# An expert stage whose matrix-engine order is written out, with whole-array work in clusters, a halved last down unit and one more raw tile

## The chip, the core and the metric

The kernel runs on one core of one Trainium2 chip. Its time is the device time of one execution in microseconds (us). The engines are TensorE (PE: matmuls; PEld: its weight loads), VectorE (DVE), ScalarE (ACT), GpSimd (POOL) and SyncE (SP), whose queue issues the loads of all weights. Lower is better; the times are medians of several runs.

## What is computed

One decoder block on 256 tokens of width 2048, with 16 meta tokens put before them: a token mixer (two attention branches, gated and merged), and after it a mixture of experts. The change touches the second part. In the reference it is

```python
g_sel = jnp.argmax(g_logits, axis=-1)                    # 1 of 4 groups for each token
top_p, top_i = lax.top_k(e_prob, TOP_K_IN_GROUP)         # 2 of the group's 4 experts
hg = jnp.einsum('td,edf->etf', t, w_gate_e)              # 16 experts, 2048 x 512 each
hu = jnp.einsum('td,edf->etf', t, w_up_e)
act = jax.nn.silu(hg) * hu * gates.T[:, :, None]
y = jnp.einsum('etf,efd->td', act, w_down_e)             # 512 x 2048 each
```

Then y is added to the residual, and a last RMS norm is taken over the rows. All is float32. The three expert matrices are 201 MB, and each is read once.

## The kernel before

**Weights.** All weights lie in DRAM as pieces of 128 x 2048 float32 (1024 KB), in the order in which they are used; 192 of them are the experts'. `Stream` (L82) hands them out. `load` (L106) issues a piece's DMA on SyncE's queue into a raw tile of the pool whose turn it is; a tile is rewritten only when what reads it is done. In the stage before the experts (L659 to L728, the output projection `wo`) the ring grows from 2 to 13 raw tiles (`MORE`, L664), and when the split pool is closed (L730) by `THIRD` = 1 more (L733): 14. In the expert stage a piece goes to PE as it is (`whole`, L125).

**Units.** The experts are taken in pairs p = 0 to 7. A pair has eight *up units* (`up_unit`, L870) and four *down units* (`down_unit`, L907), of two pieces each. Each expert holds at most 64 tokens, so its matmuls use half of the array's columns; the two of a pair of matmuls run side by side in two halves. A float32 matmul shows as two records, so that a unit has 16 records on PE. `moe_units` (L60) gives the order: the four down units of pair p - 1 stand between the up units of pair p. This order also sets that of the loads.

**Whole-array work.** Besides the units, PE has work on the full array: `gather` (L850) brings the group's tokens together, eight calls for each group of two pairs, two input chunks each, from parts that ACT and DVE make in `h_parts` (L840); `pair_map` (L821) makes the map back and the gate of each slot; `act_T` (L897) transposes the activations between the up and down units; `combine` (L920) adds a down unit's output to the residual, from a high part yh (ACT, L916) and a rest yl (DVE, L917). `combine` uses the two single PSUM tiles of `pt` and `pv`, as `pair_map` does; `act_T` uses `pt`.

**What sets the order.** The loop at L952 walks over the units. What a unit leaves to do is put off by `later` (L268) and done by `tick` (L272): `act_T` and `combine` one step after what they need. The program's order is only a priority: the framework's scheduler orders each engine's instructions by a simulation of its own, so PE's real order differs from the loop's. Each engine then works through its queue in order, as SyncE's does.

**The end.** With the last pair `combine` calls `last_sums` (L935) for each part of 512 columns: squares on ACT (L940), the product with the last gain on POOL (L941). `final_norm` (L985) takes the sums, scales the rows and stores them.

Of the kernel before, what the change touches and what calls it, by code (L numbers as in the profile page):

```python
# [8 lines left out]
F32 = mybir.dt.float32  # L9
F32R = mybir.dt.float32r  # L10
# [14 lines left out]
TAKEN = -3e38  # L25
CAP = 64
SPLITS, LOOK = 5, 3
RING, MORE, THIRD = 2, 11, 1
PIECE = 2048


# [40 lines left out]


UNITS = moe_units()
# [1 line left out]

def unit_pieces(kind, n, i):

    return (n * 12 + i, n * 12 + 4 + i) if kind == "u" else (n * 24 + 8 + i, n * 24 + 20 + i)


class Stream:  # L82
# [67 lines left out]
def hybrid_block(ctx, tc, a):  # L150
# [29 lines left out]
    def mm(out, lhsT, rhs, start, stop):  # L180
        T.matmul(out, lhsT, rhs, start=start, stop=stop, skip_group_check=True)  # L181
# [3 lines left out]
    pieces = [(W[i], PIECE) for i in range(MOE0 + 192)]  # L185
    halves = [(pieces[p], off, kp * c, False) for p, off, _, _, kp, c in HALVES]
    for u in UNITS:
        halves += [(pieces[MOE0 + i], 0, PIECE, True) for i in unit_pieces(*u)]
    st = Stream(nc, rawp, RING, splitp, halves, LOOK)


# [90 lines left out]
    def flush():  # L282
        while todo:
            tick()
# [377 lines left out]
    wr = tmp.tile([128, 16, 20], F32, name="wr")  # L662
    nc.sync.dma_start(wr, a["wr"])
    st.widen(raw2, MORE)  # L664
    hx = tmp.tile([128, 2, D], F32, name="hx")
    jq = tmp.tile([128, 128], I32, name="jq")
# [14 lines left out]
    def junk(r=128):  # L681
        return tmp.tile([128, 512], F32, name="junk", tag="junk", bufs=1)[:r]

    def y2(n):
        return tmp.tile([128, 512], F32, name="y2", tag="y2", bufs=2)

    S.activation(junk()[:, 0:1], ident[:, 0:1], AF.Sqrt)

# [178 lines left out]
    def half(e):  # L867
        return slice(64 * (e % 2), 64 * (e % 2) + 64)

    def up_unit(e, i):  # L870

        if i == 0:
            pgu[e] = psx([128, 512], "pgu")
        wg, wu = st.get()[0], st.get()[0]
        for k in range(4 * i, 4 * i + 4):
            x = XG[e // 4][k // 8][:, k % 8, (e % 4) * 64:(e % 4) * 64 + 64]
            ws = slice((k - 4 * i) * 512, (k - 4 * i) * 512 + 512)
            mm(pgu[e][half(e + 1)], x, wg[:, ws], k == 0, k == 15)
            mm(pgu[e][half(e)], x, wu[:, ws], k == 0, k == 15)
        if i == 3:  # L880
            later(0, up_out, e)

    def up_out(e):

        p = pgu.pop(e)
        if e % 2 == 0:
            act[e // 2] = moe.tile([128, 512], F32, name="act", tag="act", bufs=2)
        x = act[e // 2][half(e)]
        su = moe.tile([128, 512], F32, name="su", tag="su")[half(e)]
        S.activation(su, p[half(e + 1)], AF.Silu)  # L890
# [3 lines left out]
        if e % 2:  # L894
            later(1, act_T, e // 2)

    def act_T(p):  # L897
        q = pt([128, 4, 128], "pat")
        o = act.pop(p)
        for f in range(4):  # L900
            T.transpose(q[:, f, :], o[:, f * 128:(f + 1) * 128], ident)
        a = moe.tile([128, 4, 128], F32, name="aT", tag="aT", bufs=2)
        S.activation(a[:, 0:2, :], q[:, 0:2, :], AF.Copy)  # L903
        V.tensor_copy(a[:, 2:4, :], q[:, 2:4, :])
        aT[p] = a

    def down_unit(p, c):  # L907
# [6 lines left out]
        h = moe.tile([128, 512], F32R, name="yh", tag="yh", bufs=2)  # L914
        l = moe.tile([128, 512], F32R, name="yl", tag="yl", bufs=2)
# [4 lines left out]
    def combine(p, c, h, l):  # L920

        for t in range(2):
            q = (pv if t else pt)([128, 512], "pco")
# [3 lines left out]
            x = hh[t][:, c * 512:(c + 1) * 512]  # L927
            V.tensor_tensor(x, q, x, op=OP.add)  # L928
            if p == 7:
                last_sums(t, c)  # L930

    ssf = const.tile([128, 2, 4], F32, name="ssf")
    hgf = []

    def last_sums(t, c):  # L935

        cs = slice(c * 512, (c + 1) * 512)
        if len(hgf) <= t:
            hgf.append(unit([128, D], F32, f"hgf{t}"))
        S.activation(junk(), hh[t][:, cs], AF.Square, accum_out=ssf[:, t, c:c + 1])  # L940
        nc.gpsimd.tensor_tensor(hgf[t][:, cs], hh[t][:, cs], gfin[:, cs], op=OP.mult)  # L941

    expert_map(0)
    for k in (0, 2):
        h_parts(0, k)
    for k in range(0, 8, 2):
        gather(0, k)
        h_parts(0, k + 4)
    later(1, gate_values)
    later(2, pair_map, 0)  # L950
    nth = {}
    for kind, n, i in UNITS:  # L952
        if kind == "u":
            g, j = n // 4, n % 4 * 4 + i
            if g == 0 and j in (0, 1):
                for k in (8 + 4 * j, 10 + 4 * j):
                    gather(0, k)
                    if k < 12:
                        h_parts(0, k + 4)
            if n % 2 and i == 2 and n < 15:  # L960
                later(0, pair_map, n // 2 + 1)
            if g < 3 and j == 5:
                expert_map(g + 1)
                h_parts(g + 1, 0)
            if g < 3 and 6 <= j < 14:
                if j < 13:
                    h_parts(g + 1, 2 * (j - 5))
                gather(g + 1, 2 * (j - 6))
            if n == 13 and i == 0:
                gfin = unit([128, D], F32, "gfin")  # L970
                nc.gpsimd.dma_start(gfin, a["g_final"].to_broadcast([128, D]))
            up_unit(n, i)
        else:
            if n == 7 and i == 0:
                flush()
            down_unit(n, i)
        tick()
    flush()


    sf = const.tile([128, 2], F32, name="sf")
# [19 lines left out]
    with tc.If(more > 0):  # L1001
        with tc.tile_pool(name="fb", bufs=1) as fb:
# [16 lines left out]
            with tc.For_i(0, 16, 1) as e:  # L1019
# [22 lines left out]
                for c in range(4):  # L1042
                    y = [pj([128, 512], "pfy") for _ in range(2)]
                    nc.gpsimd.dma_start(wp, W[bass.ds(e * 12 + (MOE0 + 8 + c), 1)].rearrange("a p c -> p (a c)"))
                    for t in range(2):
                        for f in range(4):
                            mm(y[t], res[0][:, f, t * 128:(t + 1) * 128], wp[:, f * 512:(f + 1) * 512], f == 0, f == 3)
                        x = hh[t][:, c * 512:(c + 1) * 512]
                        V.tensor_tensor(x, y[t], x, op=OP.add)
            for t in range(2):  # L1050
                for c in range(4):
                    last_sums(t, c)
            final_norm()


# [5 lines left out]
def layout(i):  # L1061
# [14 lines left out]
    moe[:, 2] = f(i["w_down_e"])[0].reshape(16, 4, 128, 4, 512).transpose(0, 3, 2, 1, 4)  # L1076
    pos = np.arange(L, dtype=np.float32)[None, :]
    rope = []
    for half in (64, 32):
# [37 lines left out]
```

## Time and profile before

| | before |
|---|---|
| median of 3 runs | 1250.81 us (1250.37 to 1253.12) |
| the profiled execution | 1254.03 us |
| its span, from the first instruction to the last | 1252.4 us |
| PE busy | 1198.1 us (96%) |
| PE weight loads busy | 878.7 us (70%) |
| DVE busy | 593.5 us (47%) |
| ACT busy | 461.4 us (37%) |
| HBM read | 325.96 MB, 264 GB/s over the span |

The expert stage fills the span from about 757 us on. Matmuls overlap and their ends are modelled, so that a busy PE may still lose time at changes from one kind of work to another. The start of a matmul to the start of the next one tells more than its duration.

### The profile page before, as it was taken

The numbers are of one execution on the slowest core, as the hardware profiler recorded it, in microseconds if no ns is written. First come the engines' busy times: TensorE is split into PE (matmuls) and PEld (weight loads), VectorE is DVE, ScalarE is ACT, GpSimd is POOL, SyncE is SP. The second block draws the span as 40 slices with busy tenths as digits, with TensorE's granted clock in tenths as the row PEclk, the third lists the DMA queues.
The fourth block names the chain that finished last, engine by engine and source line by source line (L and its number), as shares of the span: only waits on it lengthen the run. The fifth ranks groups of instructions, "written<-read, shape, count | busy, mean of one in ns | idle before, by whom it ended". The sixth has DMA issues, their size and how long they took to land.

```text
span 1252.4 us, 18527 instructions
## 1 busy us (share of the span) xinstructions
PE 1198.1 (96%) x7602; PEld 878.7 (70%) x7602; DVE 593.5 (47%) x1075; ACT 461.4 (37%) x792; POOL 23.9 (2%) x31
## 2 busy tenths in 40 slices
PE   6999999999999999999999998999999999999994
PEld 6999889999999999999998875443433343333331
DVE  7768868555555655566564435232313131211212
ACT  6567644444355654444444324221211121000013
POOL 1000000000000000000000000000000000000002
PEclk9999999999999999999999998999999999999997
DMA  7554334433543444555559944999999999999992
GB/s 259 199 175 166 135 135 169 160 110 112 179 182 139 148 152 152 185 193 178 200 192 422 383 156 159 420 422 421 420 422 421 420 420 422 422 422 421 421 401 71
DMA packets 48456, 331.41 MB, mean 265 GB/s; under 512 B 5584, under 2 KB 6240, under 8 KB 9200
## 3 DMA queue, kind: packets, MB, share of 16 engines
q1 hardware_dynamic: 47088, 324.88, 66.2%
q0 software_dynamic: 1136, 5.29, 1.1%
q8 instruction: 62, 1.02, 0.3%
q14 instruction: 26, 0.21, 0.0%
q10 hardware_dynamic: 144, 0.01, 0.0%
HBM read 325.96 MB, written 4.19 MB: 264 GB/s over the span
## 4 chain that ended last, share of the span: by engine, by line
PE 92%; ACT 3%; DVE 3%; issue 1%; DMA 1%; SPq 0%; ACTq 0%
PE pj L181 50%; PE pgu L181 19%; PE py L181 10%; PE pxg L181 3%; PE pco L181 3%; PE pav L181 2%; PE pidx L181 1%; PE pqk L181 1%; ACT yh L916 1%; DVE yl L917 1%; PE prt L181 1%; DMA raw<-in_w 1%; ACT xTh L255 1%; PE psm L181 0%; DVE act L891 0%
## 5 line engine op out<-in xcount | busy, mean ns | idle before, releaser
L133 DVE TENSOR_TENSOR wlo<-raw,whi 128x1024 fp32r<-128x1024 f32 (+1 forms) x227 | 276.9, 1223 | 196.6 <-ACT whi L132 195.4
L181 PE MATMUL pj<-xTh,whi 128*128 128x256 f32 (+1 forms) x1216 | 348.0, 286 | 9.9 <-ACT xTh L255 9.9
L132 ACT ACTIVATE whi<-raw 128x1024 fp32r<-128x1024 f32 (+1 forms) x227 | 237.9, 1053 | 324.2 <-PE pj L181 297.1
L181 PE MATMUL pj<-xTl,whi 128*128 128x256 f32 (+1 forms) x1216 | 343.7, 283 | 0.0
L181 PE MATMUL pj<-xTh,wlo 128*128 128x256 f32 (+1 forms) x1216 | 342.6, 282 | 0.2 <-DVE wlo L133 0.2
L181 PE MATMUL pgu<-raw,xg 128*64 128x512 f32 x1024 | 263.2, 600 | 0.0
L181 PEld LDWEIGHTS pj<-xTh,whi 128*128 128x128 f32 x1216 | 229.5, 189 | 14.3 <-ACT xTh L255 9.9
L181 PEld LDWEIGHTS pj<-xTh,wlo 128*128 128x128 f32 x1216 | 229.1, 188 | 1.3 <-DVE wlo L133 0.5
L181 PEld LDWEIGHTS pj<-xTl,whi 128*128 128x128 f32 x1216 | 229.5, 189 | 0.7 <-issue 0.4
L181 PEld LDWEIGHTS pgu<-raw,xg 128*64 128x64 f32 x1024 | 77.8, 137 | 141.2 <-issue 137.7
L181 PE MATMUL py<-raw,aT 128*64 128x512 f32 x512 | 141.4, 603 | 0.5 <-ACT aT L903 0.5
L917 DVE TENSOR_TENSOR yl<-py,yh 128x512 fp32r<-128x512 f32 x32 | 22.1, 692 | 154.0 <-ACT yh L916 154.0
L181 PEld LDWEIGHTS py<-raw,aT 128*64 128x64 f32 x512 | 43.3, 138 | 71.1 <-issue 69.1
L916 ACT ACTIVATE yh<-py 128x512 fp32r<-128x512 f32 x32 | 19.1, 598 | 158.8 <-PE py L181 101.7
L891 DVE SCALAR_TENSOR_TENSOR act<-pgu,gsl,su 64x512 f32<-64x512 f32 x16 | 12.0, 750 | 98.7 <-ACT su L890 98.7
L890 ACT ACTIVATE su<-pgu 64x512 f32<-64x512 f32 x16 | 9.5, 592 | 131.5 <-PE pgu L181 131.5
L846 ACT ACTIVATE hsh<-hx,rh 128x256 fp32r<-128x256 f32 x64 | 30.4, 500 | 71.1 <-PE pxg L181 65.6
L847 DVE SCALAR_TENSOR_TENSOR hsl<-hx,rh,hsh 128x256 fp32r<-128x256 f32 x64 | 29.3, 479 | 49.0 <-ACT hsh L846 49.0
L181 PE MATMUL pj<-whi,mTh 128*128 128x512 f32 x128 | 51.0, 398 | 0.0
L181 PE MATMUL pj<-whi,mTl 128*128 128x512 f32 x128 | 50.5, 395 | 0.0
L181 PE MATMUL pj<-wlo,mTh 128*128 128x512 f32 x128 | 50.5, 394 | 0.0
L928 DVE TENSOR_TENSOR hx<-pco,hx 128x512 f32<-128x512 f32 x64 | 41.2, 686 | 18.5 <-PE pco L181 18.2
(293 smaller groups left out, 1389.4 us busy)
## 6 DMA issues: line engine op xcount, KB each, us to landing
raw<-in_w SPq DMA_DIRECT2D x303, 1024.0 KB, 15.7
hx<-in_x POOLq DMA_DIRECT2D x2, 1024.0 KB, 13.3
hTd<-y POOLq DMA_DIRECT2D x8, 256.0 KB, 5.5
out_dram<-hgf SPq DMA_DIRECT2D x8, 256.0 KB, 4.2
xr<-in_xT SPq DMA_DIRECT2D x3, 544.0 KB, 8.5
raw<-in_w SPq DMA_DIRECT2D x4, 256.0 KB, 7.0
raw<-in_w SPq DMA_DIRECT2D x2, 512.0 KB, 8.6
gfin<-in_g_final POOLq DMA_DIRECT2D x1, 1024.0 KB, 10.0
```

Source lines behind the costliest of these rows:

```text
L132: self.nc.scalar.activation(hi[:, c], src[:, c], AF.Copy)
L133: self.nc.vector.tensor_tensor(lo[:, c], src[:, c], hi[:, c].bitcast(F32), op=OP.subtract)
L181: T.matmul(out, lhsT, rhs, start=start, stop=stop, skip_group_check=True)
L255: S.activation(h, x, AF.Copy, scale=g)
L846: S.activation(h[:, t, :], x, AF.Copy, scale=rh[:, t:t + 1])
L847: V.scalar_tensor_tensor(l[:, t, :], x, rh[:, t:t + 1], h[:, t, :].bitcast(F32), op0=OP.mult, op1=OP.subtract)
L890: S.activation(su, p[half(e + 1)], AF.Silu)
L891: V.scalar_tensor_tensor(x, p[half(e)], gsl[e // 2][half(e)], su, op0=OP.mult, op1=OP.mult)
L916: S.activation(h, y, AF.Copy)
L917: V.tensor_tensor(l, y, h.bitcast(F32), op=OP.subtract)
L928: V.tensor_tensor(x, q, x, op=OP.add)
```

## The change

1. A context fixes PE's order in the expert stage to the order in which the program writes its instructions. The other engines are ordered by the scheduler as before. `later` and `tick` are not used in this stage any more.
2. The loop is rewritten by pairs. `beside(p)` lists the whole-array work of a pair in six clusters; `whole(k)` runs cluster k between two units, and makes the parts for the gathers of the next cluster. The order of the units is that of `moe_units` as before.
3. For pair 0 two gathers stand before each of the four up units of its first expert; before, four gathers were asked for ahead of the loop, and two more before each of the first two units.
4. The last down unit (pair 7, columns 1536 to 2047) is done in two halves of 256 columns, each with its own two loads of 512 KB, its own combine and its own last sums. For this the down weights lie in DRAM as (half, f, column) instead of (f, column), and the matmul of any down unit of 512 columns reads two runs of 256.
5. `THIRD` is 2: 15 raw tiles. The room comes from `act` and `aT`, with one buffer each instead of two, and from `wr`, `jq` and `y2`, which move to a pool that is closed before the expert stage.

```diff
-RING, MORE, THIRD = 2, 11, 1
+RING, MORE, THIRD = 2, 11, 2
...
-    return r
+    return r[:-1] + [("h", 7, 6), ("h", 7, 7)]
...
+    ph3 = ExitStack()
+    wot = ph3.enter_context(tc.tile_pool(name="wot", bufs=1, side="right"))
+    wr = wot.tile([128, 16, 20], F32, name="wr")
...
+    ph3.close()
     ph0.close()
...
 def up_unit(e, i):
...
-        if i == 3:
-            later(0, up_out, e)
...
-            act[e // 2] = moe.tile([128, 512], F32, name="act", tag="act", bufs=2)
+            act[e // 2] = moe.tile([128, 512], F32, name="act", tag="act", bufs=1)
...
-        a = moe.tile([128, 4, 128], F32, name="aT", tag="aT", bufs=2)
+        a = moe.tile([128, 4, 128], F32, name="aT", tag="aT", bufs=1)
...
-    def down_unit(p, c):
+    def down_unit(p, c, n=512):
-        w = st.get()[0], st.get()[0]
-        y = pj([128, 512], "py")
+        w = [st.get()[0].rearrange("p (h f c) -> p f h c", f=4, c=256) for _ in range(2)]
+        y = pj([128, n // 256, 256], "py")
...
-                mm(y[half(e)], aT[p][:, f, half(e)], w[e][:, f * 512:(f + 1) * 512], f == 0, f == 3)
+                mm(y[half(e)], aT[p][:, f, half(e)], w[e][:, f], f == 0, f == 3)
...
-        later(1, combine, p, c, h, l)
+        yhl[p, c] = h, l
...
+    def beside(p):
+        r = [[] for _ in range(7)]
+        if p:
+            r[0].append((act_T, p - 1))
+            for c in range(4):
+                r[2 + c].append((combine, p - 1, c, 512 * c))
+        r[2 if p == 0 else 5] += [(pair_map, 0)] if p == 0 else []
+        if p < 7:
+            r[5].append((pair_map, p + 1))
+        if p % 2 and p < 7:
+            r[0].append((expert_map, p // 2 + 1))
+            for i, k in enumerate((1, 1, 2, 2, 3, 4, 5, 5)):
+                r[k].append((gather, p // 2 + 1, 2 * i))
+        return r
+    written = tc.manual_schedule(engines={mybir.EngineType.PE})
+    written.__enter__()
     expert_map(0)
...
+    h_parts(0, 0)
+    h_parts(0, 2)
+    for p in range(8):
+        work = beside(p)
+        def whole(k):
+            for f, *x in work[k]:
+                f(*x)
+            for f, *x in work[k + 1]:
+                if f is gather:
+                    h_parts(*x)
+        def up(e, i):
+            if e == 0:
+                for k in (4 * i, 4 * i + 2):
                     gather(0, k)
                     if k < 12:
                         h_parts(0, k + 4)
+                if i == 1:
+                    gate_values()
+            up_unit(e, i)
+            if i == 3:
+                up_out(e)
...
+        up(2 * p, 0)
+        whole(0)
+        for i in range(3):
+            up(2 * p, i + 1)
+            down(i)
+            whole(i + 1)
+        up(2 * p + 1, 0)
+        down(3)
+        whole(4)
+        up(2 * p + 1, 1)
+        up(2 * p + 1, 2)
+        whole(5)
+        up(2 * p + 1, 3)
+    act_T(7)
+    down_unit(7, 0)
+    down_unit(7, 1)
+    combine(7, 0, 0, 0)
+    down_unit(7, 2)
+    combine(7, 1, 512, 1)
+    down_unit(7, 6, 256)
+    combine(7, 2, 1024, 2)
+    down_unit(7, 7, 256)
+    combine(7, 6, 1536, 3)
+    combine(7, 7, 1792, 4)
+    written.__exit__(None, None, None)
```

## Rows read from the trace of the kernel before

**Rows 1.** Waits of PE, 784 to 1240: who waited for whom, us, times, longest.

```profile
PE pco L181 <- ACT yh L916: 11.6, 17, 0.7
PE pat L901 <- DVE act L891: 5.2, 7, 1.5
PE pco L181 <- DVE yl L917: 2.6, 12, 0.2
...
PEld pgu L181 <- DMA raw<-in_w: 0.9, 3, 0.4
```

**Rows 2.** Windows: length, busy PE, PEld, DVE, ACT, POOL (count), clock, DMA share, GB/s.

```profile
768.00:772.00 4.00, 4.00 (x27) 2.48 (x26) 2.49 (x7) 2.46 (x7) 0.00 (x0) 1.00 0.17 33
772.00:776.00 4.00, 4.00 (x21) 1.34 (x20) 2.33 (x6) 3.04 (x6) 0.00 (x0) 1.00 0.95 375
776.00:780.00 4.00, 4.00 (x22) 1.79 (x24) 0.66 (x3) 0.00 (x0) 0.00 (x0) 1.00 0.91 340
780.00:784.00 4.00, 4.00 (x22) 1.36 (x20) 0.00 (x0) 0.24 (x1) 0.00 (x0) 1.00 0.99 371
...
784.00:1209.00 425.00, 408.15 (x1782) 155.95 (x1778) 104.64 (x197) 57.25 (x118) 0.54 (x1) 1.00 1.01 421
...
1208.50:1212.10 3.60, 1.65 (x10) 0.54 (x7) 0.81 (x2) 2.46 (x4) 0.00 (x0) 1.00 1.02 423
1212.10:1215.50 3.40, 3.40 (x8) 1.00 (x10) 0.38 (x1) 0.00 (x0) 0.00 (x0) 0.50 1.02 424
```

**Rows 3.** Waits of SyncE's queue, 784 to 1206.

```profile
SPq L113 <- DMA raw<-in_w: 135.5, 89, 2.1
```

**Rows 4.** SyncE's issues in the timeline; time to landing, 1196 to 1206 and whole stage.

```profile
748.31 0.33 SPq L113 DMA_DIRECT2D raw<-in_w  x1
...
770.30 1.66 SPq L113 DMA_DIRECT2D raw<-in_w  x2
...
1203.97 0.33 SPq L113 DMA_DIRECT2D raw<-in_w  x1
...
raw<-in_w SPq DMA_DIRECT2D x4, 1024.0 KB, 19.8
...
DMA to landing us min/median/max: 4.8/18.0/21.4
```

**Rows 5.** Timeline of PE, 925 to 937: start, us, what, count.

```profile
925.53 1.02 PE L181 MATMUL py<-raw,aT 128*64 128x512 f32 x2
926.48 0.39 PE L181 MATMUL pxg<-St,hsh 128*128 128x256 f32 x1
...
927.63 3.65 PE L181 MATMUL py<-raw,aT 128*64 128x512 f32 x14
...
932.06 0.73 PE L181 MATMUL pco<-yh,SgT 128*128 128x512 f32 x2
...
933.35 3.65 PE L181 MATMUL pgu<-raw,xg 128*64 128x512 f32 x14
```

**Rows 6.** Pieces of the chain that ended last, and PE's timeline at 762.

```profile
758.49 3.74 PE pxg L181 x18
...
762.16 1.08 PE L181 MATMUL pgu<-raw,xg 128*64 128x512 f32 x4
...
1102.97 0.66 PE pat L901 x4
...
1157.72 0.66 PE pat L901 x4
```

**Rows 7.** Timeline of the tail, 1195 to 1240.

```profile
1198.96 10.51 PE L181 MATMUL pgu<-raw,xg 128*64 128x512 f32 x46
...
1212.07 6.20 PE L181 MATMUL py<-raw,aT 128*64 128x512 f32 x18 [0.47 <-ACT aT L903]
...
1237.02 1.29 DVE L928 TENSOR_TENSOR hx<-pco,hx 128x512 f32<-128x512 f32 x2 [0.60 <-PE pco L181]
...
1239.32 0.16 DVE L986 TENSOR_REDUCE sf<-ssf 128x2 f32<-128x8 f32 x1 [1.01 <-ACT junk L940]
```

More of the change, by code (lines that the diff above doesn't have):

```diff
@@ L70, in moe_units @@
         r += up[6:]
-    return r
+    return r[:-1] + [("h", 7, 6), ("h", 7, 7)]
 UNITS = moe_units()
 def unit_pieces(kind, n, i):
-    return (n * 12 + i, n * 12 + 4 + i) if kind == "u" else (n * 24 + 8 + i, n * 24 + 20 + i)
+    if kind == "u":
+        return [(n * 12 + i, 0, PIECE), (n * 12 + 4 + i, 0, PIECE)]
+    if kind == "d":
+        return [(n * 24 + 8 + i, 0, PIECE), (n * 24 + 20 + i, 0, PIECE)]
+    return [(n * 24 + 12 * e + 8 + i // 2, i % 2 * PIECE // 2, PIECE // 2) for e in range(2)]
 class Stream:
@@ L187, in hybrid_block @@
     for u in UNITS:
-        halves += [(pieces[MOE0 + i], 0, PIECE, True) for i in unit_pieces(*u)]
+        halves += [((W[MOE0 + i][:, o:o + n], n), 0, n, True) for i, o, n in unit_pieces(*u)]
     st = Stream(nc, rawp, RING, splitp, halves, LOOK)
@@ L665, in hybrid_block @@
     hx = tmp.tile([128, 2, D], F32, name="hx")
-    jq = tmp.tile([128, 128], I32, name="jq")
+    jq = wot.tile([128, 128], I32, name="jq")
     nc.gpsimd.iota(jq, pattern=[[1, 128]], base=0, channel_multiplier=-1)
@@ L684, in y2 @@
     def y2(n):
-        return tmp.tile([128, 512], F32, name="y2", tag="y2", bufs=2)
+        return wot.tile([128, 512], F32, name="y2", tag="y2", bufs=2)
     S.activation(junk()[:, 0:1], ident[:, 0:1], AF.Sqrt)
@@ L893, in up_out @@
             S.activation(su[0:64, 0:1], ident[0:64, 0:1], AF.Sqrt)
-        if e % 2:
-            later(1, act_T, e // 2)
     def act_T(p):
@@ L905, in act_T, with combine @@
         aT[p] = a
-    def down_unit(p, c):
-        w = st.get()[0], st.get()[0]
-        y = pj([128, 512], "py")
+    def down_unit(p, c, n=512):
+        w = [st.get()[0].rearrange("p (h f c) -> p f h c", f=4, c=256) for _ in range(2)]
+        y = pj([128, n // 256, 256], "py")
         for f in range(4):
             for e in range(2):
-                mm(y[half(e)], aT[p][:, f, half(e)], w[e][:, f * 512:(f + 1) * 512], f == 0, f == 3)
-        h = moe.tile([128, 512], F32R, name="yh", tag="yh", bufs=2)
-        l = moe.tile([128, 512], F32R, name="yl", tag="yl", bufs=2)
+                mm(y[half(e)], aT[p][:, f, half(e)], w[e][:, f], f == 0, f == 3)
+        h = moe.tile([128, 512], F32R, name="yh", tag="yh", bufs=2)[:, :n]
+        l = moe.tile([128, 512], F32R, name="yl", tag="yl", bufs=2)[:, :n]
+        y = y.rearrange("p h c -> p (h c)")
         S.activation(h, y, AF.Copy)
         V.tensor_tensor(l, y, h.bitcast(F32), op=OP.subtract)
-        later(1, combine, p, c, h, l)
-    def combine(p, c, h, l):
+        yhl[p, c] = h, l
+    yhl = {}
+    def combine(p, c, at, last=None):
+        h, l = yhl.pop((p, c))
+        n = h.shape[-1]
         for t in range(2):
-            q = (pv if t else pt)([128, 512], "pco")
+            q = (pv if t else pt)([128, n], "pco")
             ts = slice(t * 128, t * 128 + 128)
@@ L926, in combine, with last_sums @@
             mm(q, SgT[p][:, ts], l, False, True)
-            x = hh[t][:, c * 512:(c + 1) * 512]
+            x = hh[t][:, at:at + n]
             V.tensor_tensor(x, q, x, op=OP.add)
-            if p == 7:
-                last_sums(t, c)
-    ssf = const.tile([128, 2, 4], F32, name="ssf")
+            if last is not None:
+                last_sums(t, last, at, n)
+    ssf = const.tile([128, 2, 5], F32, name="ssf")
     hgf = []
-    def last_sums(t, c):
-        cs = slice(c * 512, (c + 1) * 512)
+    def last_sums(t, i, at, n):
+        cs = slice(at, at + n)
         if len(hgf) <= t:
             hgf.append(unit([128, D], F32, f"hgf{t}"))
-        S.activation(junk(), hh[t][:, cs], AF.Square, accum_out=ssf[:, t, c:c + 1])
+        S.activation(junk()[:, :n], hh[t][:, cs], AF.Square, accum_out=ssf[:, t, i:i + 1])
         nc.gpsimd.tensor_tensor(hgf[t][:, cs], hh[t][:, cs], gfin[:, cs], op=OP.mult)
-    expert_map(0)
[L944 to L956, printed above, removed]
+    def beside(p):
[14 more added lines that the diff above has]
+    written.__enter__()
+    expert_map(0)
+    h_parts(0, 0)
[11 more added lines that the diff above has]
+                for k in (4 * i, 4 * i + 2):
                     gather(0, k)
@@ L959, in hybrid_block, with down @@
                         h_parts(0, k + 4)
[L960 to L978, printed above, removed]
+                if i == 1:
[3 more added lines that the diff above has]
+                up_out(e)
+        def down(c):
+            if p:
+                down_unit(p - 1, c)
+        if p == 6:
+            gfin = unit([128, D], F32, "gfin")
+            nc.gpsimd.dma_start(gfin, a["g_final"].to_broadcast([128, D]))
+        up(2 * p, 0)
[23 more added lines that the diff above has]
+    written.__exit__(None, None, None)
     sf = const.tile([128, 2], F32, name="sf")
@@ L1046, in hybrid_block @@
                         for f in range(4):
-                            mm(y[t], res[0][:, f, t * 128:(t + 1) * 128], wp[:, f * 512:(f + 1) * 512], f == 0, f == 3)
+                            mm(y[t], res[0][:, f, t * 128:(t + 1) * 128], wp.rearrange("p (h f c) -> p f h c", h=2, f=4)[:, f],
+                               f == 0, f == 3)
                         x = hh[t][:, c * 512:(c + 1) * 512]
                         V.tensor_tensor(x, y[t], x, op=OP.add)
+            V.memset(ssf, 0.0)
             for t in range(2):
                 for c in range(4):
-                    last_sums(t, c)
+                    last_sums(t, c, c * 512, 512)
             final_norm()
```

3 lines of the change are left out of this document (1 added, 2 removed).

## The prediction

> **What bounds the kernel now.** I read three views in this order: the waits of the matrix engine (PE), the windows with their DMA rates, and the issue times of the weight pieces. The waits say that in the expert stage PE hardly ever waits for weights: 0.9 us in all; it waits for yh and yl (11.6 and 2.6) and for act (5.2) [rows 1]. So the chain that ends last is PE's own, in an order that makes it wait for the pieces that it has just produced. The windows say that the DMA engines are as full: from 784 to 1209 they move 421 GB/s at a share of 1.01 [rows 2], and SyncE's queue issues a piece when an earlier one has landed (135.5 us in 89 waits) [rows 3]. A piece is 1.049 MB, so one lands every 1.049/0.421 = 2.49 us, and 19.8 us from issue to landing [rows 4] is eight pieces in flight. The last piece is issued at 1203.97 [rows 4], and lands at about 1223.8. Of the span of 1252.4 us, 28.6 follow that landing, because PE still has some units to do.
>
> So two limits lie close together. PE's order can be bettered by as much as it lags; after that the weights set the end, at their last landing plus a tail.
>
> **PE inside the stage.** A unit is 16 matmuls on half arrays, 14 of them in 3.0 us of starts (3.65 less the drain), so 3.43 us [rows 5]. A change to whole-array work costs: two py matmuls from 925.53 to 926.48 are 0.95 where 0.43 is the work, so 0.52 lost going in; the eight gather matmuls then take 1.15 until the next unit starts, of which I count 0.2 as lost going out (0.12 a matmul are left) [rows 5]. There are 64 such changes, counted along PE's timeline from the first units [rows 6] to the last combine (its add at 1237.02 [rows 7]); the written order has 47 by the loops of the diff: 4 in the first pass, 6 in passes 1, 3 and 5, 5 in passes 2, 4, 6 and 7, 5 at the end. That is 17 x 0.72 = 12 us. The waits for yh, yl and most of those for act go too, since a whole unit or more stands between a down unit and its combine, and between up_out and act_T: another 17 of 19.4 [rows 1]. New is a stall where pair_map takes the two PSUM tiles that the last combine has just filled: two adds of DVE, 1.29 together [rows 7], partly under the last matmuls: some 1.0 us in each of 7 passes, 7 us. PE alone would save 12 + 17 - 7 = 22 us.
>
> Check by a pass without gathers: 12 x 3.43 = 41.2, five clusters at 0.72 = 3.6, four combines of 1.29 - 0.2 = 1.1 [rows 5], 4.4, the transposes 0.66 [rows 6] and the maps about as much, stall 1.0: 51.5 us. Between two act_T now there are 1157.72 - 1102.97 = 54.8 [rows 6]. The weights of a pass need 24 x 2.49 = 59.8. So PE gets ahead of the weights, before the last pass, and then waits for them. The last up unit ends at 1209.5 now [rows 7]; PE alone would end it near 1188, the weights (below) allow 1203.9. Only 5.6 of the 22 us are needed to make the weights the bound.
>
> **The weights.** One more raw tile: one piece more is loaded before the first unit frees anything. Now the last such piece is issued at 748.31, and the next one at 770.30 [rows 4], so the tile costs nothing there and the stream after it is shorter by one piece: 2.5 us. Its lower end is 0, if the tile comes free late (it lies partly where y2 and wr were, which the router reads to the end); the pause of 22 us speaks for the full value. The tiles given up for it (a second act and aT) are rewritten a pass later, after their readers; they cost nothing, or, were that cover gone, a copy's wait of about a us a pass, inside PE's spare.
>
> The start: now 18 gather matmuls run from 758.49, the first unit begins at 762.16 [rows 6], is broken by more gathers, and ends at 770.3, when its tiles are filled anew [rows 4]. With two gathers before each of the first four units, the first ends at 762.2 + 3.6 = 765.8, the next ones each 3.43 + two gathers at 0.93 + a cluster 0.72 later, with some wait for copies: 772.2, 778.4, and 785.6 with pair_map. Data flow 1.4 us after an issue (a rate of 33 GB/s up to 772 for an issue at 770.30 [rows 2, 4]). Two pieces take 4.98, so the queue runs dry three times, and is continuous from 787.0 with 14.9 us of data moved: as if from 772.1. Now the four windows to 784 hold 4.48 MB, 10.6 us of data: as if from 773.4 [rows 2]. Gain 1.3 us, between -2 (late copies) and +3 (no gaps).
>
> So the last landing, T, is 1223.8 - 2.5 - 1.3 = 1220.0.
>
> Halving the last piece adds two transfers of the same total. With eight in flight a fixed cost of a transfer is hidden; I take nothing. Alone, a piece needs 4.8 us to land [rows 4], so 2.3 beside its data: 4.6 us for two is the upper end. The Trainium skill, DMA: Bandwidth & Descriptors, section Bandwidth, asks for at least 1 MiB in a DMA and puts lone 1 MB transfers at 341 GB/s. The trace differs for a full queue, with 421 GB/s. The reordered down weights make PE read two runs of 256 columns; no row shows that read. Between nothing and an entry of a cluster (0.52) for each of 32 units I take nothing; it lies in PE's spare, except 2 us in the last four units.
>
> **The tail.** With the weights as the bound, the last up unit's pieces land at T - 8 x 2.49 = T - 19.9; it ends at T - 16.2. From there to the first down unit is 1212.07 - 1209.47 = 2.6 [rows 7], as now, since act_T has nothing to hide behind: T - 13.6. That unit now takes some 5.4 us because the granted clock is 0.50 (1.2 GHz) from 1212.1 to 1215.5, after a gap in which PE was busy for 1.65 of 3.6 us [rows 2]; I keep this: T - 8.2. Then down 1 (3.6), combine 0 (0.52 + 1.29 [rows 5] = 1.8), down 2, combine 1, a half unit (1.8), combine 2, the last half (1.8): T + 8.0, the pieces being there each time. Combine of the first half 1.3; the last half's yh, yl and combine hide partly behind it, and its two adds of half size end at T + 11; squares, T + 11.7. From sf at 1239.32 [rows 7] to the end of the span are 13.1 us that stay. End: T + 24.8, against 28.6: 3.8 us, of which the order gives most (no yh and yl wait between down units) and the halves about 1. Its bounds: 5.7 with the clock at full, 1.5 with the two-run reads and later squares.
>
> **Sum.** 2.5 + 1.3 + 3.8 = 7.6 us. The profiled execution took 1254.03 (span 1252.4 and 1.6 around it), so 1246.4 on its scale. It stands 3.2 above the median of 1250.81; off the median the sum gives 1243.2.
>
> **Rivals.**
> PE stays the bound: if it gains under 5.6 us, the tail alone helps. From the end of the last up unit the new tail is 16.2 + 24.8 = 41.0 against 42.9 now, so 1.9, and the gain of PE on top: 1243.3 to 1248.9, say 1247. For it: PE never waits for weights now; against: 22 us worked out for 5.6 needed.
>
> Slower: written order makes each late operand stop everything behind it. Its place is each cluster, 42 of them before the last up unit. To end 2.5 us later than now, that unit must end at 1213.9, 26 us over my 1188: 0.62 us of stall in each cluster more than assumed, that is, an add of DVE waited for in full. At 0.8 us in each, 34 us, it ends at 1222, 12.5 later than now; less 1.9 of the tail that is 10.6, or 1261.4. Against: operands are a unit old (3.4 us and more), and PE's waits for them are 0.7 us at the longest even now [rows 1].
>
> The clock falls: a PE that waits for weights is granted 1.2 GHz more often. A unit of 3.43 then takes up to 6.9 (twice); but a unit's slot is 4.98, so it lags, has no more gaps, and is at full clock again, as at 1215.5. One more such spell at the end costs 1.9: 1245.1. The Trainium skill, TensorE: Matmul & The Clock Gate, section Why this matters for your kernels, warns of idle gaps between bursts of matmuls; the trace agrees, with the 0.50 after a gap.
>
> Halves land late, by 4.6 us: 1247.8. The extra tile is not there early, so that this part doesn't do what it says: 1245.7.
>
> **Chances.** What a measurement can tell from no change is about 0.2%, 2.5 us: faster is below 1248.3. Weights the bound, as summed: 0.58. PE the bound: 0.15, a third of it within 0.2%. Stalls: 0.10, slower. The clock: 0.06. The tile late: 0.05. Halves late: 0.06, half of it within 0.2%. So faster 0.58 + 0.10 + 0.06 + 0.05 + 0.03 = 0.82, same 0.08, slower 0.10. The range: the upper ends give 2.5 + 3 + 5.7 = 11.2 us, 1239.6, and 1238.0 with room for the spread of runs; at the other end it takes in PE as the bound for all but its worst case, the late tile and the late halves, to 1248.5. It leaves out the stalls.
>
> **What the profile would show.** PE waiting for raw in the last passes, tens of us instead of 0.9; about 47 changes of array use; waits of pco for yh and yl near nothing; first issue after the pause near 766; last landing near 1220, and 25 us from it to the end. Wrong if PE still shows no wait for raw (PE is the bound), if pgs, psgt or pco show long waits for DVE (stalls), or if DMA's share drops below 1 between 800 and 1200 (the first passes starve the queue).

## The result, and the profile after

The changed kernel takes 1243.17 us (median of 4 runs, 1242.56 to 1243.49); the kernel before 1251.96 (4 runs, 1250.37 to 1254.11). The ratio given with the result is 0.9925 with an interval of 0.991 to 0.9939: 8.8 us faster, on the predicted 1243.2. The profiled executions are 1254.03 and 1243.3 (spans 1252.4 and 1241.6), 10.7 apart where the sum of the prediction said 7.6. The runs of the kernel before fall into two groups by their mean granted clock, 1250.4 to 1251.7 us at 0.991 (17 of the 48 timed beside the experiments) and 1253.1 to 1255.3 at 0.988 to 0.990 (31), and its profiled execution, at 0.988, is of the second, so that part of the 10.7 is clock. So the forecast holds, but its terms need a second look.

First the pages: of the changed kernel the span and the chain that ended last by engine, then that chain of the kernel before.

```profile
span 1241.6 us, 18595 instructions
...
PE 69%; DMA 26%; DVE 2%; ACT 1%; issue 1%; SPq 0%; ACTq 0%
...
PE 92%; ACT 3%; DVE 3%; issue 1%; DMA 1%; SPq 0%; ACTq 0%
```

DMA's share goes from 1% to 26%: now a quarter of the span, some 320 us of the expert stage, runs over the arrival of weights. PE's waits in the stage, from 784 to 1242 (who waited for whom, us, times, longest), answer to [rows 1]:

```profile
PE py L185 <- DMA raw<-in_w: 6.9, 12, 1.3
PE pgu L185 <- DMA raw<-in_w: 4.2, 7, 0.7
PE psgt L835 <- DVE hx L936: 1.9, 6, 0.3
PE pat L904 <- DVE act L896: 1.5, 1, 1.5
PE pgs L185 <- DVE hx L936: 1.0, 6, 0.2
...
PEld py L185 <- DMA raw<-in_w: 20.2, 17, 2.2
PEld pgu L185 <- DMA raw<-in_w: 14.2, 14, 1.6
```

The waits of pco for yh and yl are gone, and act_T waits for act once, at the end. In their place the matmuls wait for raw for 11.1 us and their weight loads for 34.4, where it was 0.9 in all. psgt and pgs, which is pair_map behind the last combine, wait 1.9 + 1.0 us over six passes, 0.5 in each; in the kernel before the same two waits were 1.0 + 0.5.

The windows (length, busy PE, PEld, DVE, ACT, POOL, clock, DMA share, GB/s) answer to [rows 2]: the start of the stage, its whole, and the last landing.

```profile
768.00:772.00 4.00, 4.00 (x26) 2.59 (x26) 2.15 (x6) 2.43 (x6) 0.00 (x0) 1.00 0.59 227
772.00:776.00 4.00, 4.00 (x28) 2.45 (x24) 0.77 (x3) 1.01 (x3) 0.00 (x0) 1.00 0.94 344
776.00:780.00 4.00, 4.00 (x22) 1.47 (x21) 1.99 (x6) 1.42 (x4) 0.00 (x0) 1.00 0.99 416
780.00:784.00 4.00, 4.00 (x27) 2.76 (x29) 2.78 (x9) 2.69 (x7) 0.00 (x0) 1.00 0.93 352
784.00:788.00 4.00, 4.00 (x22) 1.40 (x20) 1.16 (x3) 1.61 (x2) 0.00 (x0) 1.00 0.80 291
784.00:1209.00 425.00, 409.09 (x1808) 170.30 (x1806) 103.37 (x201) 60.42 (x123) 0.54 (x1) 1.00 1.01 419
...
1220.00:1224.00 4.00, 4.00 (x31) 2.42 (x32) 2.87 (x6) 2.31 (x7) 3.14 (x3) 1.00 0.00 0
```

The stream of weights is as full as before over the stage (419 GB/s, 421 before), but it starts and ends earlier: 227 GB/s where it was 33, and nothing after 1220. The last landing, T, is at 1220.20 (1223.74 before). The 10.7 us between the two profiles are therefore 3.5 before the last landing and 7.2 behind it: 21.4 from T to the end of the span, 28.6 before.

### The profile page after: what moved, and what is told of

The parts are those of the page before. It is cut to its first block, busy times and chain, and to the rows that moved or that the text cites. A ratio compares the mean times of both kernels' runs of the same rounds, so it can differ in the third digit from the quotient of the medians.

```text
span 1241.6 us, 18595 instructions
## 1 busy us (share of the span) xinstructions
PE 1193.2 (96%) x7622; PEld 895.5 (72%) x7622; DVE 588.6 (47%) x1078; ACT 461.5 (37%) x797; POOL 24.4 (2%) x33
## 4 chain that ended last, share of the span: by engine, by line
PE 69%; DMA 26%; DVE 2%; ACT 1%; issue 1%; SPq 0%; ACTq 0%
PE pj L185 50%; DMA raw<-in_w 26%; PE pgu L185 6%; PE py L185 3%; PE pav L185 2%; PE pxg L185 2%; PE pqk L185 1%; PE pidx L185 1%; PE pco L185 1%; PE prt L185 1%; PE psm L185 0%; PE ppt L573 0%; DVE wlo L137 0%; PE ppt L571 0%; PE pvt L494 0%
## 5 line engine op out<-in xcount | busy, mean ns | idle before, releaser
L185 PE MATMUL pgu<-raw,xg 128*64 128x512 f32 x1024 | 245.3, 599 | 4.2 <-DMA raw<-in_w 4.2
L185 PEld LDWEIGHTS pgu<-raw,xg 128*64 128x64 f32 x1024 | 84.2, 137 | 135.1 <-issue 104.3
L185 PE MATMUL py<-raw,aT 128*64 128x512 f32 (+1 forms) x528 | 132.5, 583 | 7.4 <-DMA raw<-in_w 6.9
L936 DVE TENSOR_TENSOR hx<-pco,hx 128x512 f32<-128x512 f32 (+1 forms) x66 | 43.6, 670 | 186.2 <-PE pco L185 186.0
L920 ACT ACTIVATE yh<-py 128x512 fp32r<-128x512 f32 (+1 forms) x33 | 19.3, 584 | 196.1 <-PE py L185 196.1
L921 DVE TENSOR_TENSOR yl<-py,yh 128x512 fp32r<-128x512 f32 (+1 forms) x33 | 22.0, 667 | 59.4 <-ACT yh L920 59.4
L853 ACT ACTIVATE hsh<-hx,rh 128x256 fp32r<-128x256 f32 x64 | 30.4, 501 | 30.5 <-PE pxg L185 15.2
L185 PE MATMUL pj<-yah,whi 128*128 128x256 f32 x128 | 36.4, 284 | 0.0
L185 PE MATMUL pj<-yal,whi 128*128 128x256 f32 x128 | 35.9, 280 | 0.0
## 6 DMA issues: line engine op xcount, KB each, us to landing
raw<-in_w SPq DMA_DIRECT2D x6, 512.0 KB, 15.5
```

Of the source, the lines that this page charges most:

```text
L853: S.activation(h[:, t, :], x, AF.Copy, scale=rh[:, t:t + 1])
```

## The experiments

My theory after the result: from about 860 to 920 us on (the chain that ended last runs over landings from 857, PE's first waits for raw come after 900) the weights set the pace and the end, the written order gave PE some tens of us that it doesn't need, and the end is T plus a tail. The rival: PE is still the bound in most of the stage, and its waits for raw are small change. A second question is which part earned what. "Before" was timed again beside each group of runs: 1253.57 beside e1 to e4, 1253.49 beside e5 to e7, 1253.26 beside e8 to e11. The ratios of e1 to e11 are against it, that of the change against the 1251.96 of its own runs.

| run | median us | ratio (interval) | first gather | T | T to the end |
|---|---|---|---|---|---|
| before | 1253.3 to 1253.6 | | 758.49 | 1223.74 | 28.6 |
| the change | 1243.17 | 0.9925 (0.9910 to 0.9939) | 759.88 | 1220.20 | 21.4 |
| e1, one tile less | 1245.03 | 0.9937 (0.9924 to 0.9950) | 759.61 | 1222.27 | 21.5 |
| e2, last unit whole | 1241.15 | 0.9900 (0.9887 to 0.9914) | 758.17 | 1217.85 | 22.0 |
| e3, scheduler's order | 1251.52 | 0.9988 (0.9976 to 1.0000) | 759.67 | 1218.77 | 30.4 |
| e4, two experts abreast | 1241.74 | 0.9911 (0.9897 to 0.9924) | 759.93 | 1218.55 | 21.5 |
| e5, gathers twice | 1243.74 | 0.9930 (0.9913 to 0.9948) | 759.81 | 1220.76 | 21.4 |
| e6, gathers four times | 1272.22 | 1.0154 (1.0138 to 1.0171) | 760.16 | 1247.68 | 22.7 |
| e7, old loop, order fixed | 1249.91 | 0.9975 (0.9967 to 0.9984) | 758.10 | 1222.90 | 25.3 |
| e8, constants as before | 1240.37 | 0.9903 (0.9888 to 0.9918) | 757.22 | 1216.59 | 21.9 |
| e9, before, constants 32 bytes more | 1255.82 | 1.0023 (1.0011 to 1.0034) | 760.13 | 1224.14 | 28.3 |
| e10, e4 and e8 together | 1240.37 | 0.9900 (0.9885 to 0.9915) | 758.43 | 1216.11 | 23.0 |
| e11, the change again | 1243.21 | 0.9925 (0.9912 to 0.9939) | 759.29 | 1220.26 | 21.2 |

The last three columns are from each run's one profile, so a difference of a few tenths in them is not to be leaned on.

### Is a raw tile worth a piece?

```diff
-RING, MORE, THIRD = 2, 11, 2
+RING, MORE, THIRD = 2, 11, 1
```

> The changed kernel with 14 raw tiles instead of 15, the rest as it is. Theory (the weights set the end from the middle of the stage on): one piece more has to come after the pause, so the last landing and the end move by 2.49 us, from 1243.2 to 1245.7; PE waits for raw as long as before, some 30 to 45 us. Rival (PE's order sets the end, the tile is beside the point): 1243.2, the last landing unchanged against the end.

T is 2.1 us later and the time 1.9 longer, with the tail unchanged; counted from the first gather, which was 0.3 earlier, T is 2.3 later. So the extra tile is worth nearly the 2.5 us of a piece, although it is not free early: its first piece is issued only at 756.3, but the stream stands still until 768.3 anyway. It also says that T, and not PE, sets the end.

### How much can PE lose?

The loop in gather runs its matmuls again for all groups but the first (the products are written over with the same values).

```diff
-        for i in range(2):
+        for i in [0, 1] * (2 if g else 1):
```

> The changed kernel with each gather of groups 1 to 3 computed twice over on PE (the second time into the same PSUM tile, with the same result): 24 gathers, 8 matmuls of 0.12 us more in each, 22 us more of PE work in passes 1, 3 and 5. Theory (PE has more to spare than that, since it waits for raw for 30 us and more): 1243.2 to 1244.5, and the waits for raw fall by about 22 us. Rival (PE sets the end): 1265.

With e6 the same line has 4 in place of 2.

> The same, computed four times over: 67 us more of PE work. Theory: the spare is used up, waits for raw near nothing, and the end moves by what is over: 67 less 35 to 45, so 1265 to 1275. Rival (PE sets the end): 1310. A second rival (what PE waits for is not the weights but something else that grows with its work): no such knee between this run and the last.

e5 adds 192 matmuls at some 0.117 us, 22 us of PE, and the time stays: 1243.74 against 1243.17. PE's and its weight loads' waits for raw halve. The waits of e5 in the stage:

```profile
PE py L185 <- DMA raw<-in_w: 3.5, 7, 0.7
PE pgu L185 <- DMA raw<-in_w: 1.9, 3, 0.7
...
PEld py L185 <- DMA raw<-in_w: 10.3, 9, 1.6
PEld pgu L185 <- DMA raw<-in_w: 5.7, 6, 1.6
```

e6 adds 67 us, and the time grows by 29.1; of the waits for raw 1.8 us are left (a row of PEld), and the DMA share in the stage falls to 0.95, because now PE frees tiles too late. So PE has 67 - 29 = 38 us to spare in the changed kernel, and the rival is out: 22 us more work on PE cost 0.6 us on the median, and two of e5's four runs lie at 1243.6 and 1243.7.

### Is it the order or the fixing of it?

e3 takes away the three lines of the manual schedule, so that the same program is put in order by the framework's scheduler.

```diff
-    written = tc.manual_schedule(engines={mybir.EngineType.PE})
-    written.__enter__()
...
-    written.__exit__(None, None, None)
```

> The changed program, clusters, 15 tiles and halves, but PE's order left to the scheduler as in the kernel before. Theory (PE has some 15 us to spare before the weights cease to be the bound): it loses PE time, shows fewer waits for raw, but still some; the end moves by what the tail loses, 1 to 4 us: 1244 to 1247. Rival (fixing the order is all of the gain in the stage): PE is the bound again, no waits for raw, 1248 to 1250.

e7 is the kernel before, with its own loop and its planner, and only the order fixed as it issues.

```diff
+    written = tc.manual_schedule(engines={mybir.EngineType.PE})
+    written.__enter__()
     expert_map(0)
...
     flush()
+    written.__exit__(None, None, None)
```

> The kernel before, with its own loop, its 14 tiles and its whole last unit, but PE's order fixed to the order in which that program is written. Theory (weights bound once PE gains over 5 us): PE waits for raw appear, the end gains what the weights allow without the tile (no 2.5) and without the halves (no 2.3) : 1246 to 1249 against 1252. Rival (the clusters are what counts; without them the old order fixed makes PE stall as much as it gains): 1251 to 1255.

e3 loses nearly everything: 1251.52, more than theory and rival allowed, no wait of PE for raw (its weight loads 1.4 us), 30.4 us behind T, though T itself is 1.4 us earlier than in the change. e7 gains 3.6 us of the 8 to 10, between the two ranges. So the written order gains nothing to speak of unless it is fixed, and fixing the old one isn't enough. What the scheduler does to the order, a timeline of PE shows, first of e3 (start, us, what, count):

```profile
923.54 1.02 PE L185 MATMUL pgu<-raw,xg 128*64 128x512 f32 x2
924.50 0.73 PE L185 MATMUL pco<-yh,SgT 128*128 128x512 f32 x2
...
925.78 3.65 PE L185 MATMUL pgu<-raw,xg 128*64 128x512 f32 x14
929.27 1.02 PE L185 MATMUL py<-raw,aT 128*64 128x512 f32 x2
```

and then of e7 at the same place of the program, and in its last up unit:

```profile
922.11 3.65 PE L181 MATMUL pgu<-raw,xg 128*64 128x512 f32 x16
925.59 3.60 PE L181 MATMUL py<-raw,aT 128*64 128x512 f32 x16
929.93 0.50 PE L181 MATMUL pco<-yh,SgT 128*128 128x512 f32 x1 [0.73 <-ACT yh L916]
930.65 0.50 PE L181 MATMUL pco<-yl,SgT 128*128 128x512 f32 x1 [0.22 <-DVE yl L917]
...
1203.09 3.65 PE L181 MATMUL pgu<-raw,xg 128*64 128x512 f32 x14 [1.00 <-DMA raw<-in_w]
```

A down unit is eight matmuls and 16 records, so a matmul has two; two matmuls of a pair run beside each other on the array's halves. The scheduler lets one matmul of a pair, the lone x2, go ahead of the whole-array work and leaves its partner behind it. The lone one takes 923.54 to 924.50, 0.96 us, and the 14 others still take 3.5, what a whole unit of 16 takes in e7: 922.11 to 925.59. So each cut costs about 0.9 us. Ahead of whole-array work a lone x2 stands 18 times in the timeline of before, 18 times in e3, and never in e7 or in the change.

A second cost of the scheduler's order is the clock. In the kernel before a combine right behind its unit waits for yh and yl, and pair_map behind it for DVE's adds; after such a run of waits the granted clock fell in the middle of the stage:

```profile
1088.00:1092.00 4.00, 3.63 (x13) 1.53 (x15) 1.42 (x5) 0.00 (x0) 0.00 (x0) 0.65 1.01 422
1092.00:1096.00 4.00, 4.00 (x20) 1.36 (x18) 0.00 (x0) 0.00 (x0) 0.54 (x1) 0.92 1.01 420
```

That is 0.35 and 0.08 of 4 us, 1.7 us of PE. The profile of e3 has it at 1016 to 1024 (0.82 and 0.76) and 1140 to 1148 (0.68 and 0.90); those of e7 and of the change have no window of 4 us below 0.95 between 768 and their last matmul. Where PE is the bound, this counts in full: e3's times follow the mean granted clock of the run, from 1253.88 at 0.985 over 1250.7 to 1251.9 at 0.988 to 1246.57 at 0.991. So about 5 of the 8.3 us that its median loses go with the clock; that one causes the other is read from these numbers and not tried.

Why e7 doesn't gain more: the weights already bound it. Its last up unit waits 1.00 us for raw in the last row above, its matmuls wait for raw for 2.4 us and their weight loads for 10.4 in the stage, and T counted from the first gather is 464.8, as good as before's 465.3, because it has neither the extra tile nor the change's start. It gains behind T, 25.3 us for 28.6; and beside the executions of before at the clock of 0.991 (1250.4 to 1251.0) its 1249.91 gains under 1 us, so that most of the 3.6 is clock. PE isn't far ahead there: the planner puts a combine right behind its unit, the other two rows, and with the order fixed pco waits for yh and yl 30.3 us in the stage (14.2 in [rows 1]), which eats most of the 18 x 0.9 = 16 us that the whole pairs give. The old loop, fixed, with the tile and the new start was not run; so how much of the change's gain needs the clusters, and not only whole pairs, isn't shown.

### The last unit in halves

```diff
-    return r[:-1] + [("h", 7, 6), ("h", 7, 7)]
+    return r
...
-    ssf = const.tile([128, 2, 5], F32, name="ssf")
+    ssf = const.tile([128, 2, 4], F32, name="ssf")
...
-    down_unit(7, 6, 256)
-    combine(7, 2, 1024, 2)
-    down_unit(7, 7, 256)
-    combine(7, 6, 1536, 3)
-    combine(7, 7, 1792, 4)
+    down_unit(7, 3)
+    combine(7, 2, 1024, 2)
+    combine(7, 3, 1536, 3)
```

> The changed kernel with the last down unit whole again (one unit of 512 columns, two pieces, one combine). Theory (the halves shorten what follows the last landing): the last landing stays within 0.5 us of 1220.2; after it a unit of 3.5 instead of 1.9, then yh, yl, combine and adds of full size: sf some 2.3 us later, 1245.5. Rival (two more transfers and one more cluster eat it up): 1243.2 or less.

Against my expectation the kernel with the last unit whole is faster, 1241.15. The tail behaves: 22.0 against 21.4, so the halves do bring 0.6 us there. The loss is at the other end: the first gather of e2 starts at 758.17, 1.7 us before that of the change, in code that neither edit touches. From the first gather to T it takes 459.7 us, and the change 460.3. Two things were undone at once, the halves and the size of ssf, which is one of the constants at the bottom of the memory. The next pair takes them apart.

### Thirty-two bytes of constants

e8 is the change, with ssf (five columns) in a part of another constant tile that is long read by then, and a dummy of the old size in its place; e9 is the kernel before, with the larger tile and four columns of it used; e11 is the change, run once more beside them.

```diff
-    ssf = const.tile([128, 2, 5], F32, name="ssf")
+    V.memset(const.tile([128, 2, 4], F32, name="ssf"), 0.0)
+    ssf = cols[:, 40:50].rearrange("p (t c) -> p t c", t=2)
```

> The changed kernel whole, but with the ten sums of squares in unused columns of the tile cols, and the tile ssf kept at the size it had before (4 columns a half instead of 5), so that no tile on the left side of SBUF is shifted. Theory (the fifth column of ssf moved every tile after it, and PE's stream in the stages before the experts runs some 1.6 us slower for it): the first gather starts near 758.2 instead of 759.9, the end moves by as much: 1241.4. Rival (it is the 20 more PE instructions or the two more loads of the halves that delay the earlier stages): first gather at 759.9 and 1243.2.

```diff
-    ssf = const.tile([128, 2, 4], F32, name="ssf")
+    ssf = const.tile([128, 2, 5], F32, name="ssf")[:, :, 0:4]
```

> The kernel before with one edit: ssf has 5 columns a half, of which 4 are used as before. Theory (the shift of the tiles after it costs 1.6 us in the earlier stages): the first gather starts near 760.0 instead of 758.5, the wlo matmuls of the projections take some 2.5 us more in all, the time is 1.5 to 2 us over that of the kernel before. Rival (the instructions of the halves cost it): no change.

> The changed kernel once more, on the chip of these runs, to compare with: 1243.2, first gather at 759.9, last landing at 1220.2 and 21.4 from there to the end, no spell of half clock in the tail.

Eight bytes a partition more in ssf (32 as the framework pads its tiles, which no run shows by itself) cost the kernel before 0.23% (2.6 us on its median), and taking them out of the change gives 2.8: 1240.37 against 1243.21. The 2.8 may hold more than the constants: in e8's profile T also comes 0.9 us sooner behind the first gather, as the clock is back earlier there, which the part on the prediction takes up. The cost can be seen in one row of the page, matmuls of the stages before the experts (busy us and mean ns behind the bar). Of e8, with the constants as before, and of e9, with 32 bytes more:

```profile
L185 PE MATMUL pj<-xTh,wlo 128*128 128x256 f32 (+1 forms) x1216 | 342.5, 282 | 0.5 <-DVE wlo L137 0.5
```

```profile
L181 PE MATMUL pj<-xTh,wlo 128*128 128x256 f32 (+1 forms) x1216 | 345.0, 284 | 0.0
```

The same row is between 342.5 and 342.9 in the five kernels with the smaller tile (before, e2, e7, e8, e10), and between 344.9 and 345.6 in the eight with the larger. PE's order isn't the reason: up to the first gather the 5602 records of matmuls stand in the same order in before and e9, and in the change and e8. No row says which tile's new address does it.

### Filling the gaps at the start

The first pass takes its units two experts abreast, so that the gathers of an input block serve two units and frees come more evenly.

```diff
+        if p == 0:
+            r += [("u", e, i) for i in range(4) for e in range(2)]
+            continue
...
+        if p == 0:
+            for i in range(4):
+                if i == 3:
+                    pair_map(0)
+                up(0, i)
+                if i == 3:
+                    pair_map(1)
+                up(1, i)
```

> The changed kernel with the first pair's two experts taken abreast: up units (0,0), (1,0), (0,1), (1,1) and so on, the loads in the same order, so that two units and not one stand after each two gathers. Theory (the weights set the end, and the queue ran dry three times between 768 and 788): the DMA windows from 772 on are full, the last landing comes 2.5 to 4.5 us earlier, 1238.7 to 1240.7. Rival (PE sets the end): the work of PE is the same, 1243.

> Both edits that helped: the first pair's experts abreast and the sums in cols. Theory: the two gains (1.5 and 1.7) add up against the changed kernel: 1240.0, the last landing near 1217, 21.5 from there to the end. Rival (they overlap, as both let the weights start earlier): 1241.5.

In e4 the windows that ran at 344, 416, 352 and 291 GB/s in the change are full (columns as above):

```profile
772.00:776.00 4.00, 4.00 (x26) 2.47 (x27) 2.46 (x6) 2.42 (x6) 0.00 (x0) 1.00 1.01 424
776.00:780.00 4.00, 4.00 (x22) 1.40 (x20) 0.00 (x0) 0.00 (x0) 0.00 (x0) 1.00 1.02 426
780.00:784.00 4.00, 4.00 (x28) 2.48 (x26) 1.46 (x4) 2.01 (x6) 0.00 (x0) 1.00 1.01 422
784.00:788.00 4.00, 4.00 (x22) 1.31 (x20) 0.99 (x3) 0.42 (x2) 0.00 (x0) 1.00 1.01 422
```

T comes 1.65 us earlier, where I had expected 2.5 to 4.5, and the time is 1.4 us shorter, which is once more the weights as the bound. With e8 on top (e10) T counted from the first gather is again 1.7 earlier than in e8 (457.7 against 459.4), but the median is e8's, 1240.37, and the profile has a longer tail, 23.0. Its windows:

```profile
1198.00:1202.60 4.60, 2.66 (x15) 1.22 (x13) 0.90 (x2) 2.46 (x4) 0.00 (x0) 1.00 1.02 424
1202.60:1206.10 3.50, 3.50 (x10) 1.05 (x12) 0.28 (x1) 0.00 (x0) 0.00 (x0) 0.51 1.00 417
```

In this execution the first down unit met a granted clock of 0.51, 1.2 GHz, as in [rows 2]; that it is why e10 gains nothing over e8 isn't shown, and stays open: its two runs at a mean clock of 0.991 took 1239.66 and 1239.99, the two below 1240.75 and 1240.82, and e8's four, none below 0.991, lie between 1239.61 and 1241.31. Its first gather was also 1.2 us later than e8's. The best versions are e8 and e10, 1% under the kernel before and 2.8 us under the change.

## Why the prediction was right, step by step

**The weights become the bound.** Right, and with more room than I gave it. I put PE's saving at 22 us for 5.6 needed; the end of the last up unit came forward by 5.5 (1209.5 to 1203.95), and e6 shows 38 more in hand, so it is some 43. I counted the changes of array use rightly (47 for 64, by PE's timeline), and a light pass takes 48.6 us between two act_T (860.53 to 909.14) where I had 51.5 (54.8 before).

My reading of SyncE's queue was half of it. [rows 3] shows only its waits for landings; in the same stretch, 784 to 1206, it waited longer for PE to free a tile. The change turns that over. First before, then the change:

```profile
SPq L113 <- PE pgu L181: 166.2, 90, 7.9
SPq L113 <- PE py L181: 48.4, 23, 4.2
...
SPq L117 <- DMA raw<-in_w: 293.6, 142, 3.5
SPq L117 <- PE pgu L185: 49.5, 23, 5.5
SPq L117 <- PE py L185: 15.9, 18, 2.6
```

The DMA share was 1.01 either way, so the sum didn't suffer from it.

**The step that was mis-sized: "so 0.52 lost going in".** I took the two py records at 925.53 [rows 5] for one pair's work of 0.43 and a drain of 0.52. They are two records of one matmul whose partner was left for later, 2 x 0.43 and 0.1 beside it; the 14 others take 3.48, as a full unit does. The price of a real change stands in the timeline of the change, behind a unit of 16:

```profile
871.47 3.60 PE L185 MATMUL py<-raw,aT 128*64 128x512 f32 x16
875.00 0.51 PE L185 MATMUL pco<-yh,SgT 128*128 128x512 f32 x1
```

From 871.47 to 875.00 are 3.53 us for 3.43 of starts: 0.1 for going in. So 17 changes fewer are worth little (17 x 0.3 with the 0.2 going out, 5 us, not 12), and 18 cut pairs mended are worth 16. The waits for yh, yl and act that went are 15.5 up to the last up unit (the 17 that I counted take in the tail's), and pair_map's stall grew by 1.4 us, from 1.5 to 2.9 in all, and not by 1.0 in each pass. With the 1.7 of half clock at 1088 to 1096 that makes some 37 of the 43; the other 6 I have not itemised. The same error made the tail too long, below. The order of size was right for the wrong reason; the 3.43 of a unit stands, though it was read from such a run of 14. The two prices are read from timelines; no run changes the number of switches alone.

**The weights' term.** T was to be 1220.0 and is 1220.20, but by two errors that cancel. The stage begins 1.4 us later than before (first gather 759.88, not 758.49), which I had not foreseen: it is the constants, as e9 shows with 1.6. From the first gather T comes 4.9 us earlier, not 3.8. The tile gave 2.3 (e1; 2.5 predicted). The rest is the start: the five windows from 768 to 788 hold 6.52 MB, 15.5 us at 421 GB/s, so the stream is as if from 772.5, 12.6 us behind the first gather, where it was 773.4 and 14.9: 2.3 us, not 1.3. The first issue after the pause is at 768.26, 8.4 behind the first gather, where I had 7.3 (765.8). The 1.0 is the clock: the gathers and the first 2.1 us of the first unit ran at a granted clock of 0.50, 1.2 GHz (0.79 is the mean of 764 to 768, so it rose at about 765.7). I hadn't carried that beyond the gathers; the unit took 4.60 us (763.57 to 768.17) and not 3.6. In e8 the clock was back as the unit began, and it took 3.58. The change, its window, and e8:

```profile
763.57 4.67 PE L185 MATMUL pgu<-raw,xg 128*64 128x512 f32 x16
...
764.00:768.00 4.00, 4.00 (x16) 1.03 (x12) 1.76 (x6) 0.94 (x3) 0.00 (x0) 0.79 0.00 0
...
760.67 3.65 PE L185 MATMUL pgu<-raw,xg 128*64 128x512 f32 x16
```

The queue runs dry thrice as foreseen; those are the dips of the windows, and e4 puts their price at 1.7.

**The halves and the two-run reads cost nothing in the stream.** Right. The changed kernel's issues between 1197 and 1206 (count, size, us to landing):

```profile
raw<-in_w SPq DMA_DIRECT2D x4, 512.0 KB, 16.8
```

These four land at 1216.45, 1217.68, 1218.95 and 1220.20, 1.25 apart, half of 2.49: no fixed cost shows beside the data, and the last one has landed before the last half unit (below) begins. The rival with 4.6 us is out. The Trainium skill, DMA: Bandwidth & Descriptors, section Bandwidth, asks for 1 MiB or more in a DMA; with eight in flight the trace shows no loss at half of that. And py's units of 16, reading two runs of 256 columns, are followed by the next work 3.53 us after their start, the pgu units of one run by theirs after 3.43 to 3.58.

**The tail.** Right in its parts up to the first down unit, too long behind it: 24.8 predicted, 21.4 measured. The timeline of the change:

```profile
1206.55 7.34 PE L185 MATMUL py<-raw,aT 128*64 128x512 f32 x32 [0.47 <-ACT aT L906]
1213.82 0.51 PE L185 MATMUL pco<-yh,SgT 128*128 128x512 f32 x1
...
1218.82 0.51 PE L185 MATMUL pco<-yh,SgT 128*128 128x512 f32 x1
...
1221.84 0.51 PE L185 MATMUL pco<-yh,SgT 128*128 128x512 f32 x1
...
1222.98 1.95 PE L185 MATMUL py<-raw,aT 128*64 128x256 f32 x16
1224.86 0.38 PE L185 MATMUL pco<-yh,SgT 128*128 128x256 f32 x1
...
1228.22 0.16 DVE L1034 TENSOR_REDUCE sf<-ssf 128x2 f32<-128x10 f32 x1 [0.73 <-ACT junk L948]
```

The first down unit starts at T - 13.65 (13.6 predicted). Two units then take 7.27, where I had 5.4 + 3.6 = 9.0: the spell of half clock, which I kept, did not come, 1.8 us. A combine and a unit take 5.00 (5.4), a combine and a half 3.02 (3.6), twice: 1.6 us together, the drain of 0.52 again. The last unit ends at T + 4.7 for T + 8.0. I had named full clock as a bound, 5.7 for 3.8; the measured 7.2 lies outside it, by the mis-sized drain.

**The range and the chances.** The case that I held likeliest, weights as the bound, came. Stalls in written order, the slower rival, didn't: psgt's and pgs's longest wait is 0.3 us. That the median meets 1243.2 to 0.03 us is luck: on the profiled pair the tail gave 3.4 us more than I said and T 0.3 less, 10.7 for 7.6; on medians the gain is 8.8, 1.2 more than the sum, and the median of before is now 1251.96, 1.2 above the 1250.81 from which I took it off. What lies between the two ways of counting is the clock of before's runs: the profiled one has half clock twice behind 784, at 1088 to 1096 and in the first down unit.

## What to carry to other kernels

Where two limits lie close, work out what each alone would allow, and spend effort on the one that is left: here PE got 43 us and 5.5 of them counted, while a tile and a fuller start, some 2 us each, and a tail shorter by 7 all count in full. Before pricing a switch of modes from a short run of records, see whether the run is whole: a lone x2 beside an x14 is a cut pair, and the remedy is to keep the pair together, not to switch less often. And when an edit to the end of a kernel shifts the constants, compare the first stages too: unchanged code that runs slower there is part of the price.

## What the runs showed of the hardware that I had not expected

**An address can cost.** Thirty-two bytes more in the constants made matmuls of unchanged stages slower, 345 us instead of 342.5 for 1216 of one kind, and the kernel by 2.6 to 2.8 us (e9, e8). Which of the shifted tiles it is, and by what, was not tried.

**The clock after one and the same gap.** Behind the last up unit PE has the same wait for act in all these kernels. In the profile of the kernel before the granted clock fell to 0.50 behind it [rows 2], and in those of e3 (0.54) and e10 (0.51 in the window above). In the change it stayed at 1.00, in e9, which is the kernel before but for 32 bytes, and in the eight others. The windows of the change:

```profile
1202.00:1206.50 4.50, 2.60 (x13) 1.10 (x9) 0.76 (x1) 2.46 (x4) 0.00 (x0) 1.00 1.01 422
1206.50:1210.00 3.50, 3.45 (x16) 1.20 (x17) 0.42 (x1) 0.00 (x0) 0.00 (x0) 1.00 1.01 420
```

2.60 of 4.50 us busy there, and 2.66 of 4.60 in e10: nothing in these rows tells the two apart. In e9 the rows ahead are even those of before, 1.65 us busy of 3.60. The Trainium skill, TensorE: Matmul & The Clock Gate, section Why this matters for your kernels, warns of idle gaps between bursts of matmuls; here the same gap had the penalty of 1.8 us in some executions and not in others, so it is a chance and not a fixed term, and the prediction should have carried it as one.
